# Local-attention scores at the head of a step, and transposes copied by two engines in turn

## The chip, the cores and the metric

The kernel runs on one core of one Trainium2 chip. The metric is the device time of a whole launch in microseconds. The version before the change takes 2577.65 us (median of 3 runs, 2576.64 to 2578.03). A core has a matrix engine (TensorE, "PE" in the profile, with its weight loads shown as "PEld"), VectorE (DVE), ScalarE (ACT), GpSimd (POOL) and SyncE (SP), which issues nearly all DMAs here. TensorE writes to PSUM, of which there are eight banks; DVE and ACT read PSUM and write SBUF.

## The reference, cut to what matters

Two layers on 512 tokens of width 1024. Each layer is a SwiGLU block, a token mix of three attention branches, and a second SwiGLU block, each followed by a layer norm. The change touches the token mix alone.

```python
def _token_mix(h, w_in, ...):
    q_a, kv_a, g_a, q_b, k_b, v_b, q_c, k_c, v_c, f_c = _split_cols(h @ w_in)
    o_a = _nsa(q_a, kv_a, g_a, ...)      
    o_b = _swa_sink(q_b, k_b, v_b, sinks, ...)  
    o_c = _fox(q_c, k_c, v_c, f_c, b_f)  
    g = jax.nn.sigmoid(h @ w_gate + b_gate).reshape(B, S, N_BRANCH, D)
    merged = g[:, :, 0] * (o_a @ w_br_a) + g[:, :, 1] * (o_b @ w_br_b) + g[:, :, 2] * (o_c @ w_br_c)
    return merged @ w_out
```

`_swa_sink` is local attention: a query block of 128 tokens sees its own block and the one before, with a bias and a sink in the softmax. `_fox` is causal attention with a decaying bias over all earlier blocks. `_nsa` has a compressed branch (its keys and values come from a small two-layer network over 32-token blocks, called the conv here), a selected branch and a window branch; with 512 tokens all eight blocks of 64 are selected, so both see all earlier tokens. Eight heads each, 64 wide, in pairs.

## The kernel before

All matrix products are done at nearly fp32 accuracy: a weight tile `raw` arrives by DMA, ACT rounds it to `hi` (L140), DVE forms the rest `lo` (L141), and one k of a projection is three matmuls of 512 columns (L161 to L163). The order of TensorE's and POOL's instructions is the order in which the program writes them; those of ACT, DVE and SP are ordered by the compiler's scheduler.

In `mix` (once per layer) the projections of the token mix are cut into *fillers*: `chunk` makes eight of them out of one projection of 128 columns, one per k, and appends them to the deque `fill`. `pump(n)` runs the next n. When the last filler of a chunk has run, its `then` starts the evacuation: `set_q` has ACT and DVE build a query tile `qs` in four instructions in turn (L403, L404) and makes the query known to the order two fillers or more later; `fox_k` and `nsa_k` build key tiles `ks` through DMAs; `set_v` transposes values. Entries marked `free` don't count: among them `feed`, which stands ahead of the fillers from the third query chunk on and issues the two loads of one conv weight `cw1` (L529) as long as fewer than four are under way. Other fillers are `m.cum` (a cumulative sum by matmuls, L483 and L486), `tr` (transposes `glT` in the conv, L550) and `conv2` (its last products `kv`, L582 and L585).

The attention is done by *units*: `Swa`, `Fox` and `Nsa`, each for one pair of heads and one query block. A unit has three parts:

- `s`, scores: matmuls into a PSUM tile of tag `sc` (three buffers), then bias, maximum, exponential and scale on DVE, ACT, and POOL or DVE (`norm`, L610). The result is `p`, in SBUF. It yields once for each of `nseg` segments: one for `Swa`, two for `Fox` and `Nsa`.
- `tr`, transposes: TensorE transposes `p` block by block into a PSUM tile of tag `tp` (two buffers; names ptS, ptF, ptN, ptC), and `ev_pt` copies each back to `p`. It yields after each group; `ngrp` is their number: one for `Swa`, two for `Fox`, three or five for `Nsa`.
- `pv`: the products with the values into one PSUM tile `po`.

`ev_pt(dst, src, n)` raises a counter that all callers share and gives the copy to DVE (L393) when n divides the counter, otherwise to ACT (L395); n = 0 is always ACT, and n = 1, for Nsa's compressed tile ptC, always DVE. The transposes of values (`vT`) use n = 2.

SBUF tiles of tag `p` have PB = 13 buffers: scores, the conv's inputs `z` (four), its weights `cw1` and `cw2`, and small ones such as `gl`, which holds the forget gate's logarithms until `cum` has run.

There are eight batches with two `Swa` units each, then for each of four head pairs one batch with four units and two with two. `step(cur, prev, n)` weaves three things into TensorE's stream: the scores of the batch `cur`, the transposes of the batch before (`prev`), and n fillers; then it does `pv` for `prev`, and behind it what `feed` has put into `narrow`, the conv's matmuls `hid` (L536). It first pumps until the queries and keys of `cur` exist. Two fillers are kept for the time between the last transposes and `pv`. The rest is spread over `slots`, the larger of the numbers of score segments `ns` and pairs of transpose groups `nt`; in a slot the scores come first, then fillers up to the slot's middle, then a pair of transpose groups, then fillers up to its end. For a Swa step ns was 2 and nt 1: two slots, the transposes in the second. `PUMPS` lists n for every step.

Of the kernel before, what the change touches and what calls it, by code (L numbers as in the profile page):

```python
# [18 lines left out]
P = 128  # L19
# [45 lines left out]
def body(tc, a, out, depth=DEPTH):  # L65
# [15 lines left out]
    def ps(tag=None, name="ps", shape=(P, 512)):  # L81
        if tag is None:
            tag = PS_ALL[ring[0] % 8]
            ring[0] += 1
        return psp.tile(list(shape), F32, name=name, tag=tag, bufs=PS_TAGS[tag])
# [266 lines left out]
    def mix(l, wts, pend, done_ffn, xap, xa, nxt):  # L352
# [35 lines left out]
        def ev_pt(dst, src, n):  # L388

            eng[0] += 1  # L390
            with tc.high_priority(100):
                if n and eng[0] % n == 0:
                    nc.vector.tensor_copy(dst, src)  # L393
                else:
                    nc.scalar.activation(dst, src, AF.Copy)  # L395
# [118 lines left out]
        def conv(ws):  # L514
# [52 lines left out]
            def end():  # L567
                while narrow or c.n < 16:
                    feed()
                    narrow.popleft()()  # L570
                tr()
# [40 lines left out]
        class Swa:  # L612
# [37 lines left out]
            def tr(u):  # L650
                pv = u.p.rearrange("p s (b q) -> p s b q", q=P)[:, :, 0:u.nb]
                pt = ps("tp", "ptS", (P, 2, 2, P))[:, :, 0:u.nb]
                for s in range(2):
                    for b in range(u.nb):
                        nc.tensor.transpose(pt[:, s, b], pv[:, s, b], ident)
                ev_pt(pv, pt, 4)
                yield

            def pv(u, po):
# [7 lines left out]
        class Fox:  # L667
# [33 lines left out]
            def tr(u):  # L701
                n = u.qb + 1
                for s in range(2):
                    pt = ps("tp", "ptF")[:, 0:n * P]
                    for b in range(n):
                        nc.tensor.transpose(pt[:, b * P:(b + 1) * P], u.p[s][:, b * P:(b + 1) * P], ident)
                    ev_pt(u.p[s][:, 0:n * P], pt, 0)
                    yield

            def pv(u, po):  # L710
# [6 lines left out]
        class Nsa:  # L717
# [83 lines left out]
            def tr(u):  # L801
                for s in range(2):
                    for p in u.n[s]:
                        pt = ps("tp", "ptN", (P, 2, 2, P))[:, 0:p.shape[1]]
                        for k in range(p.shape[1]):
                            for br in range(2):
                                nc.tensor.transpose(pt[:, k, br], p[:, k, br], ident)
                        ev_pt(p, pt, 3)
                        yield
                    if s == 0:  # L810
                        pc = u.pc.rearrange("p s n -> p (s n)")
                        pt = ps("tp", "ptC", (P, P))
                        nc.tensor.transpose(pt, pc, ident)
                        ev_pt(pc, pt, 1)
                        yield
# [100 lines left out]
        def pump(n=1):  # L916
            while n > 0 and fill:
                n -= fill.popleft()() is not FREE
# [30 lines left out]
        chunk(CKV + 2 * P, nsa_k(0))  # L949
        chunk(CKV + 4 * P, nsa_k(1))  # L950
        fill.append(tr)
        chunk(CQA, set_q(m.qa, 0))
        fill.insert(len(fill) - 2, lambda: conv2(cv))
# [23 lines left out]
        def need(u):  # L977
            if u.br == 1:
                return u.m in m.qb and hasattr(m, "kb")
            if u.br == 2:  # L980
                return u.m in m.qc and u.m in m.kc and u.m in m.vc and u.m in m.nck
            return u.m in m.qa and hasattr(m, "vbd") and hasattr(m, "kc2")
# [8 lines left out]
        def chain(gens):  # L991
            for g in gens:
                yield from g

        def step(cur, prev, n):


            for u in cur:
                while not need(u):
                    pump(1)  # L1000
                    n -= 1
            it, iu = chain(u.tr() for u in prev), chain(u.s() for u in cur)
            nt, ns = sum(u.ngrp for u in prev), sum(u.nseg for u in cur)
            pair = 2
            nt = (nt + pair - 1) // pair
            slots = max(nt, ns, 1)
            done = 0

            def upto(x):
                nonlocal done  # L1010
                x = int(round(x))
                if x > done:
                    pump(x - done)
                    done = x

            last = min(2, max(n, 0))
            n -= last
            for j in range(slots):
                if j * ns // slots != (j + 1) * ns // slots or slots == ns:
                    next(iu, None)  # L1020
                upto(n * (2 * j + 1) / (2 * slots))
                if j * nt // slots != (j + 1) * nt // slots or slots == nt:
                    for _ in range(pair):
                        next(it, None)
                upto(n * (j + 1) / slots)
            for _ in iu:
                pass
            for _ in it:
                pass
            pump(last)  # L1030
            if prev:
                po = ps("po", "po", (P, 4, P))
                for j, u in enumerate(prev):
                    u.pv(po[:, j])
                while narrow:
                    narrow.popleft()()
                for j, u in enumerate(prev):
                    nc.scalar.activation(o_t[u.br][u.m][:, u.qb * P:(u.qb + 1) * P], po[:, j], AF.Copy)

        PUMPS = [10] * 8 + [11, 10, 11] * 4 + [8]  # L1040
        for cur, prev, n in zip(batches + [[]], [[]] + batches, PUMPS):
            step(cur, prev, n)
        while fill:
# [40 lines left out]
        for d in range(KD):  # L1084
            g_t = gates0 if d == 0 else g_1 if d == 1 else gates(d)
            for br in (1, 2, 0):
# [3 lines left out]
                p = ps(name="brp")  # L1090
# [114 lines left out]
    for l in range(depth):  # L1205
        fin = l == depth - 1
        wts, pend, done = ffn(l, a["ffn1_w1"][l], a["ffn1_w2"][l], 0, xa, wts, pend, done, False, lambda: mix_first(l))
        wts, pend, done, xap, xa = mix(l, wts, pend, done, xap, xa, lambda: ffn_first(a["ffn2_w1"][l]))
        wts, pend, done = ffn(l, a["ffn2_w1"][l], a["ffn2_w2"][l], 2, xa, wts, pend, done, fin,
                              lambda: None if fin else ffn_first(a["ffn1_w1"][l + 1]))  # L1210
# [30 lines left out]
```

## Time and profile before

| | |
|---|---|
| median of the runs | 2577.65 us |
| the profiled execution's own time | 2576.7 us |
| its span, first to last instruction | 2575.0 us |
| granted TensorE clock, mean | 0.998 |
| DMA, mean | 104 GB/s, 268.97 MB |
| Swa steps of the first layer | about 428 to 517 us |
| Fox and Nsa steps of the first layer | about 517 to 712 us |
| the same of the second layer | about 1704 to 1793 and 1793 to 1988 us |

A row such as `458.52 0.63 PE L655 MATMUL ptS<-ident,p ... x4 [0.84 <-ACT p L395]` is read: at 458.52 us from the span's start, for 0.63 us, four matmuls of line 655 write ptS from ident and p; TensorE was idle 0.84 us before, until ACT's instruction of line 395 on tile p ended. In a list of groups, the busy time in us and the mean of one in ns stand between the two bars, and the idle time before the group with its releasers behind the second.

### The profile page before, as it was taken

What the parts mean: (1) busy time and instruction counts of PE and PEld (TensorE: products, weight loads), DVE (VectorE), ACT (ScalarE), POOL (GpSimd) and SP (SyncE); (2) the same over time, 40 slices, a digit from 0 to 9 for tenths busy, and PEclk for the clock granted to TensorE, in tenths of its full rate; (3) what the DMA queues carried; (4) which work ended last, traced back from release to release, by engine and by line L of the source; (5) the groups of instructions that cost most, each with busy time, mean ns of one, the idle gap of its engine ahead of it and who ended that gap; (6) DMA issues with size and microseconds to landing.
All of it is one profiled execution on the core that took longest, in us unless ns stands there. A gap on an engine that the chain in (4) does not pass through costs nothing. (4 is left out here: it accounts for less than half of the span.)

```text
span 2575.0 us, 34112 instructions
## 1 busy us (share of the span) xinstructions
PE 2544.7 (99%) x13099; PEld 2109.3 (82%) x13099; DVE 1197.1 (46%) x2565; ACT 949.3 (37%) x1947; POOL 184.4 (7%) x371
## 2 busy tenths in 40 slices
PE   9999999999999999999999999999999999999998
PEld 8888887788888888888888888877888888888887
DVE  4344245576654363332343432555766534543323
ACT  3222224477642332222232221345776323322211
POOL 0000001133300000000000000101332000000000
PEclk9999999999999999999999999999999999999999
DMA  6433334633143433333333332435321434233331
GB/s 213 119 94 95 98 92 127 172 82 83 50 139 99 122 99 98 98 98 92 113 90 98 96 94 97 129 102 156 95 75 42 143 103 142 81 97 98 99 92 63
DMA packets 375170, 268.97 MB, mean 104 GB/s; under 512 B 17384, under 2 KB 351272, under 8 KB 375008
## 3 DMA queue, kind: packets, MB, share of 16 engines
q1 hardware_dynamic: 373856, 262.61, 35.0%
q0 software_dynamic: 1152, 4.19, 0.4%
q8 instruction: 103, 1.69, 0.3%
q14 instruction: 59, 0.48, 0.1%
HBM read 247.83 MB, written 9.49 MB: 100 GB/s over the span
## 5 line engine op out<-in xcount | busy, mean ns | idle before, releaser
L141 DVE TENSOR_TENSOR lo<-raw,hi 128x1024 fp32r<-128x1024 f32 (+2 forms) x414 | 490.8, 1189 | 854.4 <-ACT hi L140 853.8
L140 ACT ACTIVATE hi<-raw 128x1024 fp32r<-128x1024 f32 (+2 forms) x414 | 424.4, 1031 | 1226.0 <-issue 696.4
L161 PE MATMUL pj<-xh,hi 128*128 128x512 f32 (+1 forms) x720 | 267.2, 371 | 1.5 <-ACT vt L448 1.4
L163 PE MATMUL pj<-xh,lo 128*128 128x512 f32 (+1 forms) x720 | 254.9, 354 | 0.4 <-DVE lo L141 0.4
L162 PE MATMUL pj<-xl,hi 128*128 128x512 f32 (+1 forms) x720 | 254.7, 354 | 0.0
L161 PE MATMUL pg<-xh,hi 128*128 128x512 f32 x640 | 249.7, 390 | 0.0
L162 PE MATMUL pg<-xl,hi 128*128 128x512 f32 x640 | 249.7, 390 | 0.0
L163 PE MATMUL pg<-xh,lo 128*128 128x512 f32 x640 | 249.5, 390 | 0.0
L163 PE MATMUL pu<-xh,lo 128*128 128x512 f32 x640 | 249.0, 389 | 0.0
L161 PE MATMUL pu<-xh,hi 128*128 128x512 f32 x640 | 249.0, 389 | 0.0
L162 PE MATMUL pu<-xl,hi 128*128 128x512 f32 x640 | 249.0, 389 | 0.0
L174 PE MATMUL acc<-hi,ha 128*128 128x512 f32 x576 | 227.3, 395 | 0.0
L175 PE MATMUL acc<-hi,ha 128*128 128x512 f32 x576 | 227.3, 395 | 0.0
L176 PE MATMUL acc<-lo,ha 128*128 128x512 f32 x576 | 227.2, 395 | 0.0
L286 DVE TENSOR_TENSOR t<-t,pu 128x512 f32<-128x512 f32 x80 | 55.0, 687 | 216.6 <-PE pu L163 216.6
L163 PEld LDWEIGHTS pj<-xh,lo 128*128 128x128 f32 x720 | 135.5, 188 | 20.5 <-DVE lo L141 0.6
L161 PEld LDWEIGHTS pj<-xh,hi 128*128 128x128 f32 x720 | 136.0, 189 | 17.0 <-issue 3.1
L162 PEld LDWEIGHTS pj<-xl,hi 128*128 128x128 f32 x720 | 136.2, 189 | 11.3 <-DVE xl L1187 0.2
L203 POOL TENSOR_SCALAR st<-st 128x1 f32<-128x1 f32 x24 | 8.4, 352 | 1890.4 <-ACT junk L201 1890.4
L163 PEld LDWEIGHTS pg<-xh,lo 128*128 128x128 f32 x640 | 120.6, 188 | 25.1
L162 PEld LDWEIGHTS pg<-xl,hi 128*128 128x128 f32 x640 | 120.5, 188 | 25.0
L161 PEld LDWEIGHTS pg<-xh,hi 128*128 128x128 f32 x640 | 120.5, 188 | 25.0
(244 smaller groups left out, 4322.9 us busy)
## 6 DMA issues: line engine op xcount, KB each, us to landing
raw<-in_ffn_w_dram SPq DMA_DIRECT2D x264, 512.0 KB, 3.8
raw<-in_w_in_dram SPq DMA_DIRECT2D x56, 512.0 KB, 4.0
raw<-in_w_gate_dram SPq DMA_DIRECT2D x48, 512.0 KB, 3.9
ks<-hl SPq DMA_DIRECT2D x96, 128.0 KB, 2.3
raw<-in_w_out_dram SPq DMA_DIRECT2D x16, 512.0 KB, 3.7
tab<-bvec SPq DMA_DIRECT2D x16, 256.0 KB, 2.8
x_sp<-xa POOLq DMA_DIRECT2D x8, 512.0 KB, 6.8
cw<-in_cmp_k_w_dram SPq DMA_DIRECT2D x32, 128.0 KB, 3.5
```

The lines of the kernel that those rows point to most:

```text
L140: nc.scalar.activation(hi[:, c], raw[:, c], AF.Copy)
L141: nc.vector.tensor_tensor(lo[:, c], raw[:, c], hi[:, c].bitcast(F32), op=OP.subtract)
L161: nc.tensor.matmul(o, hi[:, k], vh, start=first, stop=False)
L162: nc.tensor.matmul(o, hi[:, k], vl, start=False, stop=False)
L163: nc.tensor.matmul(o, lo[:, k], vh, start=False, stop=last)
L174: nc.tensor.matmul(o, sh(k)[:, t], hi[:, c], start=k == 0, stop=False)
L175: nc.tensor.matmul(o, sl(k)[:, t], hi[:, c], start=False, stop=False)
L176: nc.tensor.matmul(o, sh(k)[:, t], lo[:, c], start=False, stop=k == nk - 1)
L203: nc.gpsimd.tensor_scalar(st[:, 4:5], st[:, 3:4], 1.0 / D, EPS / ALPHA ** 2, op0=OP.mult, op1=OP.add)
L286: nc.vector.tensor_tensor(t, t, pu, op=OP.mult)
```

## The change

Three things, all in `mix`. The `n` of `ev_pt` becomes 2 for the transposes of all three kinds of units (before: 4 for Swa, 0 for Fox, 3 for Nsa; ptC keeps 1, vT its 2). In `step`, where the current batch has exactly two score segments in all, which is a batch of two Swa units, both are issued in one go: ns is halved, so there is one slot in place of two, with both scores at its head and the transposes in its middle. And `PUMPS` gives the first two steps 13 fillers in place of 10, the next six 9 in place of 10; their sum stays 80.

```diff
@@ Swa.tr
-                ev_pt(pv, pt, 4)
+                ev_pt(pv, pt, 2)
@@ Fox.tr
-                    ev_pt(u.p[s][:, 0:n * P], pt, 0)
+                    ev_pt(u.p[s][:, 0:n * P], pt, 2)
@@ Nsa.tr
-                        ev_pt(p, pt, 3)
+                        ev_pt(p, pt, 2)
@@ step
             nt = (nt + pair - 1) // pair
+            both = 2 if ns == 2 else 1
+            ns //= both
             slots = max(nt, ns, 1)
...
                 if j * ns // slots != (j + 1) * ns // slots or slots == ns:
-                    next(iu, None)
+                    for _ in range(both):
+                        next(iu, None)
...
-        PUMPS = [10] * 8 + [11, 10, 11] * 4 + [8]
+        PUMPS = [13, 13] + [9] * 6 + [11, 10, 11] * 4 + [8]
```

## The prediction

> **What bounds the kernel now.** I read the page's busy rows first, then the list of what TensorE waited for, then the two attention stages of each layer as windows, and last the order of instructions around each wait.
>
> ```profile
> PE 2544.7 (99%) x13099; PEld 2109.3 (82%) x13099; DVE 1197.1 (46%) x2565; ACT 949.3 (37%) x1947; POOL 184.4 (7%) x371
> ```
>
> TensorE is busy for 2544.7 of 2575.0 us. No edit takes a matmul away, so what can be won is TensorE's idle time, 30.3 us in all, and only the part that the change touches. The list of TensorE's waits (engine, line, what it waited for: us in total, times, longest) has all that matters:
>
> ```profile
> PE ptN L807 <- ACT p L395: 5.8, 8, 1.7
> ...
> PE sS L629 <- DVE qs L404: 2.7, 2, 1.3
> PE glT L550 <- DVE p L393: 1.7, 2, 0.9
> PE ptS L655 <- DVE p L610: 1.7, 2, 0.9
> PE ptS L655 <- ACT p L395: 1.7, 2, 0.8
> PE ptC L813 <- ACT p L395: 1.4, 2, 0.7
> ```
>
> Each comes an even number of times: once or more per layer, in the same place. The windows of the two layers bear this out (columns: PE, weight loads, DVE, ACT, POOL busy, granted clock, DMA share, GB/s). The first and third are the Swa steps, the others the Fox and Nsa steps:
>
> ```profile
> 420.00:517.00 97.00, 92.13 (x555) 71.62 (x552) 62.62 (x203) 50.73 (x142) 11.28 (x24) 1.00 0.57 155
> 517.00:712.00 195.00, 191.40 (x1431) 160.43 (x1432) 131.83 (x573) 136.26 (x458) 66.94 (x127) 1.00 0.26 70
> 1696.00:1793.00 97.00, 92.12 (x555) 71.74 (x553) 62.66 (x202) 50.77 (x142) 11.23 (x24) 1.00 0.57 155
> 1793.00:1988.00 195.00, 191.39 (x1432) 160.46 (x1433) 131.39 (x574) 136.40 (x459) 66.85 (x127) 1.00 0.26 70
> ```
>
> TensorE sits idle 4.9 us in a layer's Swa steps and 3.6 us in its Fox and Nsa steps; the clock is full. Whatever I work out for one layer counts twice.
>
> The list shows a little less than a wait costs, because a matmul's recorded end lies past the start of its successor when nothing stops it:
>
> ```profile
> 441.17 0.39 PE L163 MATMUL pj<-xh,lo 128*128 128x512 f32 x1
> 441.40 0.38 PE L655 MATMUL ptS<-ident,p 128*128 128x128 f32 x2
> 442.63 0.41 PE L655 MATMUL ptS<-ident,p 128*128 128x128 f32 x2 [0.85 <-DVE p L610]
> ```
>
> The first takes 0.39 us and the next starts 0.23 us after it, so 0.16 us is overlap. I add 0.16 us to every listed wait.
>
> **The order of the Swa steps, counted out.** A filler is one k of a projection, three matmuls of 0.23 us or 0.69 us. The fillers of a layer are numbered from the first step: 1 is the last of zk, 2-9 zv, 10-17 the second q chunk (qb1), 18-25 qb2, 26 `cum`, 27-34 qb3, 67 `tr`, 74 `conv2`. Before, a Swa step is: scores, 4 fillers, scores, 2 fillers, both transposes, 2 fillers, 2 more, then the products with v. After, it is both scores, 4 fillers (6 in the second step), both transposes, the other fillers, products. `both` acts only where two Swa units are current, which is eight steps; the sum of fillers is 80 in both versions, so from the ninth step on the order is the same. Steps 1 and 2 end at fillers 13 and 26 instead of 10 and 20.
>
> **Waits that this removes.**
>
> First, the transposes of the second step (the 0.85 us row above) stand behind a softmax scale that is late because DVE works through zv's additions. Scores to transposes: 12 fillers before; now scores at filler 0, transposes after filler 19. At 0.69 us that is 4.8 us more, which exceeds the wait. Removed: 1.7 + 2x0.16 = 2.0 us.
>
> Second, the third step's scores want qb1, which is made by ACT and DVE in turn after filler 17:
>
> ```profile
> 448.63 0.44 PE L629 MATMUL sS<-ks,qs 128*128 128x128 f32 x2
> 450.40 0.44 PE L629 MATMUL sS<-ks,qs 128*128 128x128 f32 x2 [1.33 <-DVE qs L404]
> ...
> 449.66 0.69 DVE L404 SCALAR_TENSOR_TENSOR qs<-pj,qs 64x512 fp32r<-64x512 f32 x1
> ```
>
> Before, step 3 starts at filler 20, three fillers later; now at filler 26, nine later, 4.1 us more. Removed: 2.7 + 2x0.16 = 3.0 us.
>
> Third, `cum` was filler 26 and lay just ahead of step 3's transposes, so three tiles asked for two `tp` buffers:
>
> ```profile
> 456.71 0.38 PE L483 MATMUL cum<-tri,gl 128*8 128x128 f32 x2
> 457.02 0.33 PE L655 MATMUL ptS<-ident,p 128*128 128x128 f32 x1
> ...
> 458.52 0.63 PE L655 MATMUL ptS<-ident,p 128*128 128x128 f32 x4 [0.84 <-ACT p L395]
> ```
>
> Now `cum` ends step 2 and four fillers, products and scores come before the next transposes. Removed: 1.7 + 2x0.16 = 2.0 us. Together **-7.0 us**.
>
> `tr`, filler 67, stays directly behind a step's transposes (step 7 is 63-71, its transposes after 66), and those were copied by ACT and DVE already (counts 11 and 12 of the shared counter, every fourth to DVE). I leave the 1.7 us of glT as they are.
>
> **Waits that it may add in the Swa steps.** The pool `p` has 13 buffers. In step 2, z holds 4, cw2 1, gl 1 (until `cum`), the four score tiles 4: three are left, and a step takes up to four conv weights (`feed`, from filler 18 on). Before, only three fillers of step 2 came after that point; the fourteenth tile was a score tile of step 3, and it did wait for `cum`:
>
> ```profile
> 457.69 0.42 DVE L605 CUSTOM_DVE_ANT_0 p<-sS,tab 128x256 f32<-128x256 f32 x1
> ...
> 461.83 1.09 PE L663 MATMUL po<-p,v 128*64 128x128 f32 x16
> 462.75 1.90 PE L536 MATMUL hid<-cw,z 128*64 128x256 f32 x16
> ...
> 448.38 0.51 SPq L529 DMA_DIRECT2D cw<-in_cmp_k_w_dram  x1
> 449.23 0.34 SPq L529 DMA_DIRECT2D cw<-in_cmp_v_w_dram  x1
> ...
> cw<-in_cmp_k_w_dram SPq DMA_DIRECT2D x16, 128.0 KB, 3.3
> cw<-in_cmp_v_w_dram SPq DMA_DIRECT2D x16, 128.0 KB, 2.8
> ```
>
> DVE wrote that score tile 0.7 us after `cum` had ended near 457.0, and TensorE never felt it. Now step 2 has fillers 18 to 26, so the fourteenth can be the fourth conv weight, whose load can start only when `cum` ends at the tail of step 2. Its second half is issued 0.85 us after its first and lands 2.8 us later, 3.65 us after `cum`. TensorE wants it after the products (0.92 us) and three quarters of a hid group (three quarters of 1.83), 2.3 us after `cum`. In the worst case it stands 1.35 us per layer, and what is queued behind it is TensorE's whole stream; in the best case a score tile waits again (0). I take the middle, 0.7: **+1.4 us**, ends 0 and 2.7. Later steps are one conv group earlier and have free buffers. The other loads of SP keep their order of need; a filler's weights are fetched a chunk ahead.
>
> `conv2` (filler 74) takes a `tp` buffer:
>
> ```profile
> 511.07 0.68 PE L585 MATMUL kv<-cw,glt 128*64 128x64 f32 x8
> ...
> 512.36 0.55 ACT L593 ACTIVATE vbd<-kv 32x128 f32<-32x128 f32 x2 [0.35 <-POOL vbd L579]
> ```
>
> It is read out 1.2 us after its matmuls end (512.91 against 511.75). Before, scores and two fillers lay between it and the transposes; now one filler, 0.69 us. The first transposes have the other buffer and take 0.4 us, so the second are short by 0.1 us at best, and by 1.3 us if the last two exponentials of that step's scores go ahead of it on ACT. I take 0.5: **+1.0 us**, ends 0 and 2.6.
>
> **The copies.** In the Fox and Nsa steps of one layer, 517 to 712 us (groups by line: busy us, mean ns of one, then the engine's idle time before them):
>
> ```profile
> L395 ACT ACTIVATE p<-ptF 128x128 f32<-128x128 f32 (+3 forms) x32 | 13.1, 432 | 7.9 <-PE ptF L706 6.6 <-POOL p L610 0.9
> L395 ACT ACTIVATE p<-ptN 128x512 f32<-128x512 f32 (+1 forms) x30 | 15.5, 516 | 5.6 <-PE ptN L807 5.5
> L393 DVE COPY p<-ptN 128x512 f32<-128x512 f32 (+1 forms) x18 | 10.8, 601 | 3.5 <-PE ptN L807 2.0 <-POOL p L610 1.3
> ```
>
> Counting through, 16 of the 32 ptF copies and 15 of the 30 ptN copies go to DVE, and 9 of the 18 go back to ACT; ptC (n = 1) stays on DVE and moves the shared counter on, so there are runs of three on one engine. ACT loses 6.6 + 7.8 and gains 4.7 us: 127 of 195. DVE gains 16.7 and loses 5.4 us: 143 of 195, the fuller of the two. The longest wait shows why ACT alone was late, and how DVE can be:
>
> ```profile
> 615.77 0.27 PE L813 MATMUL ptC<-ident,pc 128*128 128x128 f32 x1
> 617.69 0.52 PE L807 MATMUL ptN<-ident,p 128*128 128x128 f32 x3 [1.64 <-ACT p L395]
> ...
> 616.96 0.58 ACT L395 ACTIVATE p<-ptN 128x512 f32<-128x512 f32 x1
> ...
> 615.89 1.22 DVE L141 TENSOR_TENSOR lo<-raw,hi 128x1024 fp32r<-128x1024 f32 x1
> ...
> 617.45 0.28 DVE L393 COPY pc<-ptC 128x128 f32<-128x128 f32 x1
> ```
>
> All ten waits here (8 ptN, 2 ptC) are for an ACT copy: 7.2 + 10x0.16 = 8.8 us is the most that can go, 0 the least. With two buffers and alternate engines each run of three still has one copy on ACT, and the tile after it waits for that one; only the waits in which two ACT copies queued up shrink. I take half: **-4.4 us**. Against it stand copies that now queue behind a weight split on DVE; I take +1.0 us, from 0 to 3.7 (62 moved copies of both layers, a tenth of the window in such splits, 0.6 us left of one).
>
> A repeated gap on TensorE before a tile of two buffers bears on a rule of the Trainium skill (Perfetto Trace Analysis, Optimization Strategy): the same gap repeated on the engine that should be full can mean too few buffers for the next tile. By it the copier matters little, this term is 0 and the time that of the second rival below.
>
> **Sum:** -7.0 + 1.4 + 1.0 - 4.4 + 1.0 = -8.0 us. The profiled execution took 2576.7 us, 1.7 over its span and 0.95 under the median; 2568.7 for it is **2569.6 us** as a median.
>
> **Rivals.**
>
> All attacked waits go and none comes: -7.0 - 8.8, 2561.8 us. For it: ACT is the only releaser in the second stage. Against: ACT keeps half the copies.
>
> The copies win nothing, the two buffers being the cause: -7.0 + 2.4 + 1.0, 2574.0 us. For it: the wait at 617.69 is for one of a pair, and the pair's other copy will now be on ACT.
>
> Slower: DVE becomes what releases the `tp` buffers. Place: the Fox and Nsa steps. Mechanism: a copy stands behind a weight split, as the ptC of 615.77 did, copied 1.4 us after its matmul. If a quarter of the 62 moved copies are so late and TensorE stands 1.2 us for each, 15x1.2 = 18 us; with the Swa terms 2577.65 - 7.0 + 2.4 + 18 = 2591 us. It cancels the Swa gain from four such waits on, and shows as slower from nine. For it: DVE at 143 of 195 us. Against: no wait of TensorE in these steps is for DVE today, though it does 18 such copies and 16 of ptC per layer.
>
> A copy is also longer on DVE:
>
> ```profile
> L395 ACT ACTIVATE p<-ptN 128x512 f32<-128x512 f32 x40 | 23.6, 589 | 8.7 <-PE ptN L807 8.5
> ...
> L393 DVE COPY p<-ptN 128x512 f32<-128x512 f32 x24 | 16.6, 690 | 6.3 <-PE ptN L807 4.0 <-POOL p L610 1.3 <-POOL pc L610 1.0
> ```
>
> That is 0.10 us for the largest form, 6.3 us over 62 copies, of which the sum has none on TensorE's path, since DVE's 52 idle us a layer hold it. The Trainium skill (Perfetto Trace Analysis, Optimizing Scalar/DVE Operations) speaks against the move likewise: it puts the fixed cost of reading PSUM at about 125 ns on DVE and 51 on ScalarE. By those 74 ns, all on the path, 4.6 us (an estimate) would come off the gain, which would leave 3.4.
>
> **How the numbers follow.** 0.2% (5.2 us) is about what a measurement of this kernel tells from no change. Forecast 0.54, all waits gone 0.12, copies win nothing 0.23, slower 0.11. The first two are faster by more than that (below 2572.5) save for 0.02 of the forecast's own spread; the third is within it; the fourth above. So faster 0.64, same 0.25, slower 0.11. The forecast's own range is 2564 to 2575; the whole range goes from the second case (2561) to 2579, past the third with all its unknown costs at their upper ends (2574.0 + 1.3 + 1.6 + 2.7 = 2579.6).
>
> **What would show it.** In the changed profile the three Swa waits (ptS for L610, sS for L404, ptS for L395) are gone and glT's stays; a wait of hid L536 for a cw load shows the fourteenth buffer, one of ptS L655 near conv2's kv the `tp` clash. ptN and ptC waits for ACT about halve, with small ones for DVE copies at their side. DVE's busy time in the Fox and Nsa window is near 143 us and ACT's near 127. Wrong would be: DVE as releaser of most ptN waits, or a Swa window that still has more than 4 us idle.

## The result, and the profile after

The changed kernel takes 2569.17 us (median of 7 runs, 2565.98 to 2569.57). In the same comparison the kernel before takes 2576.47 us (7 runs, 2576.09 to 2578.03). The ratio is 0.9968, with a 95% interval of 0.9957 to 0.9980: faster by about 7 us. 2569.6 us was forecast. The profiled execution took 2569.09 us, against 2576.7 before.

The span is 2567.4 us. The matmuls are the same 13099 and are busy for 2545.5 us, as long as before (2544.7), so the time came out of TensorE's idle time. Its list of waits, after (us in total, times, longest):

```profile
PE ptN L807 <- DVE pc L393: 3.0, 2, 1.5
PE glT L550 <- DVE p L393: 1.7, 2, 0.9
...
PE ptS L655 <- ACT p L395: 0.9, 2, 0.5
PE ptN L807 <- ACT p L395: 0.9, 2, 0.5
PE ptC L813 <- ACT p L395: 0.4, 2, 0.2
```

The two waits of the Swa steps for L610 and L404 are not in it. glT's 1.7 us stand as before. What ptN and ptC waited for ACT copies was 5.8 + 1.4 us and is 0.9 + 0.4. But 3.0 us of ptN now stand under a DVE copy, ptS waits for an ACT copy in a new place, and a wait of hid for a load (0.2 us) is new. The two windows of the first layer that the prediction shows, after:

```profile
420.00:517.00 97.00, 94.57 (x574) 73.49 (x573) 63.74 (x209) 49.86 (x141) 13.98 (x26) 1.00 0.57 155
517.00:712.00 195.00, 192.76 (x1434) 162.03 (x1434) 139.96 (x594) 129.70 (x441) 65.67 (x125) 1.00 0.26 72
```

TensorE's idle time fell from 4.9 to 2.4 us in the one and from 3.6 to 2.2 us in the other. Windows at fixed times shift against the work when a kernel gets faster, so from here on a stage is cut where its work begins: the Swa stage from its first sS to the first sF, the Fox and Nsa stage from there to the first brp, in both layers. Before (the first number behind the window is its length; the row left out has 90.23 again):

```profile
428.51:518.74 90.23, 86.03 (x536) 67.56 (x535) 59.03 (x194) 47.94 (x138) 12.07 (x26) 1.00 0.57 155
518.74:718.11 199.37, 195.77 (x1446) 164.06 (x1445) 133.90 (x577) 140.70 (x467) 66.14 (x126) 1.00 0.26 70
...
1794.97:1994.10 199.13, 195.52 (x1446) 164.07 (x1445) 133.25 (x577) 140.62 (x467) 66.06 (x126) 1.00 0.26 71
```

and after:

```profile
429.93:517.60 87.67, 85.92 (x536) 67.76 (x535) 59.02 (x198) 44.99 (x134) 13.98 (x26) 1.00 0.59 161
517.60:715.18 197.58, 195.34 (x1447) 164.18 (x1445) 142.62 (x598) 132.52 (x445) 65.67 (x125) 1.00 0.25 71
1701.80:1789.08 87.28, 85.87 (x535) 67.75 (x534) 58.96 (x198) 44.99 (x134) 14.03 (x26) 1.00 0.59 161
1789.08:1986.66 197.58, 195.34 (x1446) 164.20 (x1445) 141.99 (x598) 132.66 (x445) 65.75 (x125) 1.00 0.26 71
```

The Swa stages won 2.56 + 2.95 = 5.5 us, the Fox and Nsa stages 1.79 + 1.55 = 3.3 us, 8.85 us together. The span fell by 7.6 us only. 1.4 of these were lost long before the changed code: the first Swa stage begins at 429.93 in place of 428.51. The windows of the same ten microseconds, before and then after, show it:

```profile
36.00:46.00 10.00, 10.00 (x48) 7.57 (x48) 6.39 (x10) 2.04 (x3) 0.00 (x0) 0.83 0.61 172
```

```profile
36.00:46.00 10.00, 10.00 (x40) 6.60 (x40) 6.38 (x10) 2.02 (x3) 0.00 (x0) 0.66 0.62 177
```

The granted clock was 0.66 in place of 0.83, so that 40 matmuls were done and not 48. The kernels do the same work there. In the profiles of before, after and the experiments below, which (but for the third `tp` buffer) differ in the token mix alone, the first Swa stage begins anywhere from 426.7 to 430.5 us, so this varies from execution to execution. The stage lengths leave it out; the totals don't.

### The profile page after: what moved, and what is told of

Same layout as the page of the kernel before. It is cut to its first block, busy times and chain, and to the rows that moved or that the text cites. A ratio compares the mean times of both kernels' runs of the same rounds, so it can differ in the third digit from the quotient of the medians.

```text
span 2567.4 us, 34066 instructions
## 1 busy us (share of the span) xinstructions
PE 2545.5 (99%) x13099; PEld 2110.8 (82%) x13099; DVE 1214.1 (47%) x2617; ACT 927.4 (36%) x1895; POOL 187.6 (7%) x371
## 4 chain that ended last, share of the span: by engine, by line
PE 97%; DVE 1%; ACT 1%; DMA 1%; issue 0%; POOL 0%; DVEq 0%; POOLq 0%; SPq 0%; ACTq 0%
PE acc L176 7%; PE acc L174 7%; PE acc L175 7%; PE pg L161 6%; PE pg L162 6%; PE pg L163 6%; PE pu L161 6%; PE pu L163 6%; PE pu L162 6%; PE pj L161 5%; PE pj L163 5%; PE pj L162 5%; PE gate L161 3%; PE gate L162 3%; PE gate L163 3%; PE brp L162 2%
## 5 line engine op out<-in xcount | busy, mean ns | idle before, releaser
L141 DVE TENSOR_TENSOR lo<-raw,hi 128x1024 fp32r<-128x1024 f32 (+2 forms) x414 | 490.3, 1188 | 852.0 <-ACT hi L140 851.3
```

The lines of the kernel that those rows point to most:

```text
L141: nc.vector.tensor_tensor(lo[:, c], raw[:, c], hi[:, c].bitcast(F32), op=OP.subtract)
```

## The experiments

Two theories were set against each other part by part. Mine was that of the prediction: the order and the fillers win in the Swa stage, the copies win in the Fox and Nsa stage, and the parts add up. The rivals were that only one part does the work, and that the two `tp` buffers, not the copying engine, set the waits.

**The copies alone** (kernel before, all three `ev_pt` with n = 2):

```diff
-                ev_pt(pv, pt, 4)
+                ev_pt(pv, pt, 2)
-                    ev_pt(u.p[s][:, 0:n * P], pt, 0)
+                    ev_pt(u.p[s][:, 0:n * P], pt, 2)
-                        ev_pt(p, pt, 3)
+                        ev_pt(p, pt, 2)
```

> Only the three ev_pt counts become 2; order and PUMPS as before. Theory (each edit acts in its own stage): TensorE's waits in the Fox and Nsa steps go as in the changed kernel, ptN and ptC standing 2.7 us a layer instead of 4.4, the Swa waits (ptS, sS, glT) stay; 3 to 4 us faster than before. Rival 1 (the order earns all of it, the copies nothing): Fox and Nsa waits unchanged within 0.5 us, time within 1 us of before. Rival 2 (DVE becomes the releaser): ptN waits for DVE copies of more than 5 us in all, slower.

Measured: 2576.20 us against 2576.99, ratio 0.9995 (0.9986 to 1.0004). No gain could be measured. The stage windows of this kernel say why:

```profile
428.13:518.88 90.75, 86.23 (x535) 67.55 (x534) 61.50 (x198) 46.02 (x134) 12.07 (x26) 1.00 0.57 155
518.88:716.51 197.63, 195.39 (x1446) 164.21 (x1445) 142.90 (x599) 132.50 (x445) 65.95 (x126) 1.00 0.26 71
1703.50:1795.81 92.31, 87.83 (x535) 68.70 (x534) 61.47 (x198) 46.01 (x134) 12.02 (x26) 0.98 0.56 152
```

In the Fox and Nsa stages the whole gain is there: 1.74 us here, 1.55 in the second layer's (197.58 us). The Swa stages gave back 0.5 and 2.1 us, and in the second layer the clock is at 0.98. The 0.5 us, in both layers, lies at step 2's products, which wait for a copy on DVE, and just ahead of step 3's scores. TensorE's timeline at step 3's scores in the second layer (the first layer's row, at 450.57, has the same 1.37 us):

```profile
1725.93 0.44 PE L629 MATMUL sS<-ks,qs 128*128 128x128 f32 x2 [1.37 <-DVE qs L404]
```

and the window just behind it:

```profile
1726.00:1730.00 4.00, 4.00 (x12) 3.19 (x13) 1.45 (x9) 0.97 (x5) 0.59 (x2) 0.57 0.90 273
```

There the clock fell to 0.57. In the first layer the same wait left it at 1.00 over the whole stage: the 1.6 us between the two Swa stages (92.31 and 90.75) are the price of the clock. So the copies are worth 3.3 us in one stage, and in this kernel the old Swa steps give most of it back.

**The order and the fillers, with the old copies** (the changed kernel, with n back at 4, 0 and 3):

> Both scores at the head and the new PUMPS; the copy counts as before (4, 0, 3). Theory: the three Swa waits (ptS for L610, sS for L404, ptS for L395 behind cum) go, small ones come (hid for a cw load, ptS behind conv2's kv), the Fox and Nsa waits stay at 4.4 us a layer; 5 to 6 us faster than before. Rival 1: the whole 8 us. Rival 3 (the Swa waits only move): under 2 us faster.

Measured: 2571.82 us, ratio 0.9981 (0.9973 to 0.9990), 5.2 us faster. The first layer's stages of this kernel:

```profile
426.72:514.25 87.53, 85.81 (x535) 67.77 (x534) 56.44 (x194) 46.93 (x138) 12.00 (x26) 1.00 0.59 160
514.25:713.65 199.40, 195.81 (x1447) 164.00 (x1445) 133.62 (x577) 140.59 (x467) 65.98 (x125) 1.00 0.25 70
```

The Swa stage is as short as in the changed kernel, the other as long as before. In this kernel each part keeps to its stage.

**The order alone** (the same, with PUMPS as before):

```diff
-        PUMPS = [13, 13] + [9] * 6 + [11, 10, 11] * 4 + [8]
+        PUMPS = [10] * 8 + [11, 10, 11] * 4 + [8]
```

> Only both scores at the head of a Swa step; PUMPS and copies as before. Theory: step 3 starts at filler 20 again, so sS still waits 1.5 us a layer for the query; cum, filler 26, now comes two fillers behind the transposes and its wait goes; tr, filler 67, comes three fillers behind them and the 1.0 us of glT go; conv2, filler 74, stands directly ahead of the transposes of step 8, which then wait 1 to 2 us. 1 to 3 us faster in all. Rival 4 (the order is what earns the Swa part): 5 us or more faster.

Measured: 2581.13 us, ratio 1.0016 (1.0007 to 1.0025): slower, against my expectation. The waits of the transposes in steps 2 and 3 and that of glT are gone, as expected. The waits for the queries are not. TensorE's timeline at step 3's scores in the first layer:

```profile
449.76 0.44 PE L629 MATMUL sS<-ks,qs 128*128 128x128 f32 x2 [1.94 <-DVE qs L404]
451.98 1.65 PE L629 MATMUL sS<-ks,qs 128*128 128x128 f32 x6 [1.77 <-DVE qs L404]
```

and the window behind them:

```profile
453.00:457.00 4.00, 4.00 (x12) 3.23 (x12) 2.17 (x16) 2.05 (x10) 0.23 (x1) 0.51 0.98 307
```

Step 3's scores stood 3.7 us a layer for the query, where 1.35 were listed before, and the clock fell to 0.51 behind them. Two reasons can be read off, counted from the first sS (428.51 before, 429.34 here). The stand in step 2 that the order removes had been time for the query too: TensorE is free for step 3's scores 1.5 us sooner. And the query is ready 0.7 us later (its last instruction on DVE ends at 451.92 here, at 450.35 before): ACT begins it at 448.42, behind all four exponentials of step 2, where it began at 445.22, ahead of them. Together that is the 2.3 us by which a layer's wait grew.

**The fillers alone** (kernel before, with the new PUMPS):

> Only the new PUMPS; two slots and the copy counts as before. Theory: the query wait of step 3, the late softmax of step 2 and the clash of cum with step 3's transposes all go by the filler numbers alone, hid waits for a cw load as in the changed kernel (0.3 to 0.7 us a layer), conv2 lies four fillers' work ahead of the transposes and costs nothing: 5 to 7.5 us faster than before, as much as order and fillers together or more. Rival 4: under 3 us faster.

Measured: 2572.54 us, ratio 0.9980 (0.9971 to 0.9989). Its Swa stages:

```profile
429.81:517.62 87.81, 85.99 (x536) 67.83 (x535) 59.36 (x194) 47.50 (x138) 14.57 (x26) 1.00 0.60 162
...
1704.05:1791.43 87.38, 85.85 (x536) 67.83 (x535) 59.46 (x194) 47.51 (x138) 14.60 (x26) 1.00 0.60 163
```

That is 175.2 us for both, and 175.1 with order and fillers: on top of the fillers, scores at the head add nothing. The six more fillers ahead of step 3 are what wins in the Swa stage, since they alone remove the wait for the query.

**One conv weight fewer at the start** (the changed kernel):

```diff
-                if c.n < 16 and len(narrow) < 4:
+                if c.n < 16 and len(narrow) < (3 if c.n <= 3 else 4):
```

> The changed kernel, but feed gives step 2 only three conv weights, so that no fourteenth tile asks for a buffer of p before cum has run. Theory (the wait of hid in step 2 is the fourteenth buffer): no hid wait for a cw load is left, the Swa stage of the first layer (first sS to first sF) is 0.6 us shorter than the changed kernel's 87.67, that of the second 0.3 shorter than 87.28. Rival (the loads are late for another reason, the DMA queue): hid still waits.

Measured: 2576.89 us, ratio to the kernel before 0.9997 (0.9987 to 1.0007), so the gain was gone. TensorE's timeline of this kernel in the first layer:

```profile
451.41 1.46 PE L536 MATMUL hid<-cw,z 128*64 128x256 f32 x12
...
503.77 0.61 PE L550 MATMUL glT<-ident,gl 128*128 128x128 f32 x2 [2.32 <-DVE gl L544]
```

and the window that begins at the second row:

```profile
503.00:508.00 5.00, 4.23 (x13) 3.45 (x14) 1.11 (x4) 0.17 (x1) 0.00 (x0) 0.66 1.20 229
```

The three weights of step 2 ran without a stand, so the fourth is the cause there. That it is its buffer, the changed kernel's list of what SP waited for shows; neither the kernel before nor this one has such a row:

```profile
SPq L529 <- PE cum L483: 6.8, 2, 3.4
```

But one weight was then left over for a step of its own, its load was late (1.28 us), `tr` waited 2.32 us for the conv's result, and the clock fell. The test answers its question, and its total says nothing about the price of the wait.

**The conv's last products two fillers earlier** (the changed kernel):

```diff
-        fill.insert(len(fill) - 2, lambda: conv2(cv))
+        fill.insert(len(fill) - 4, lambda: conv2(cv))
```

> The changed kernel with conv2 two fillers earlier, so that three fillers and not one lie between kv and the transposes of step 8. Theory (the ptS wait there is kv still holding a tp buffer): the 0.64 us of ptS go in both layers, Swa stages 0.6 us shorter. Rival (the copies of the transposes themselves are late): ptS still waits.

Measured: 2570.71 us, ratio 0.9973 (0.9962 to 0.9984). The wait near kv did not move. Timelines of TensorE, ACT and POOL of this kernel:

```profile
511.83 0.38 PE L655 MATMUL ptS<-ident,p 128*128 128x128 f32 x2
512.68 0.66 PE L655 MATMUL ptS<-ident,p 128*128 128x128 f32 x4 [0.47 <-ACT p L395]
...
515.27 0.53 ACT L593 ACTIVATE vbd<-kv 32x128 f32<-32x128 f32 x2
...
512.66 1.40 POOL L610 TENSOR_SCALAR p<-p,stS 128x256 f32<-128x256 f32 x3 [9.64 <-ACT p L395]
514.01 0.30 POOL L579 MEMSET vbd<- 128x256 f32 x1
```

kv's buffer is held until ACT has read it into vbd, and that waits for vbd's memset on POOL, which stands in program order behind the scales of both scores. So the second transposes take the buffer of the first, and wait for ACT's copy of these. Moving the matmuls of kv doesn't free the buffer.

**All copies to one engine** (the changed kernel with n = 1 for all three, and with n = 0 for all three; ptC stays on DVE in both):

> The changed kernel with every copy of a transpose of the three units on DVE. Theory (a late copy costs on whichever engine it queues, and two engines are better than one): ptN waits for DVE of 2 to 5 us a layer, Fox and Nsa stage (first sF to first brp) 198 to 201 us against 197.58. Rival (ACT's lateness was the whole cause): no ptN wait left, stage under 196.5.

> The changed kernel with every copy of a transpose of the three units on ACT (ptC stays on DVE). Theory: ptN waits for ACT of more than 4.4 us a layer, Fox and Nsa stage 199.5 to 202 us; Swa stage within 1 us of the changed kernel's. Rival (the number of tp buffers is the cause, not the copier): stage within 0.5 us of 197.58.

Measured: all on DVE 2572.07 us, ratio 0.9977 (0.9968 to 0.9987); all on ACT 2577.07 us, 0.9999 (0.9989 to 1.0008). The first Fox and Nsa stage, all on DVE:

```profile
517.53:716.34 198.81, 196.21 (x1446) 164.30 (x1445) 160.74 (x639) 116.48 (x404) 64.81 (x125) 1.00 0.26 70
```

with this wait at the head of those in the stage:

```profile
PE sN L765 <- DVE stN L605: 1.8, 2, 0.9
```

The same stage, all on ACT:

```profile
518.61:720.20 201.59, 197.52 (x1446) 165.32 (x1445) 123.93 (x558) 147.97 (x486) 67.07 (x125) 0.99 0.25 70
```

and its largest wait there:

```profile
PE ptC L813 <- ACT p L395: 5.0, 6, 1.7
```

The stage goes 201.6, 198.8 and 197.6 us for all on ACT, all on DVE and in turn. On ACT the copies come late themselves. On DVE they come mostly in time (ptN waits 1.5 us for them in the whole list), but sN now waits for the softmax on DVE that frees its `sc` buffers, 3.4 us in the whole list: most of the wait moved from transposes to scores.

**A third `tp` buffer**, taken from the scores (the changed kernel):

```diff
-    PS_TAGS = {"mm": 2, "sc": 3, "tp": 2, "po": 1}
+    PS_TAGS = {"mm": 2, "sc": 2, "tp": 3, "po": 1}
```

> The changed kernel with three PSUM buffers for transposes and two for scores. Theory of the two buffers (the second rival of the prediction: not who copies but how many tiles wait): the ptN and ptC waits of the Fox and Nsa stage go almost wholly, 2.7 us a layer; but scores may wait for their own two, so that the stage is 195 to 199 us. Theory of the copier: a third buffer leaves more than 1 us a layer of ptN waits. The Swa stage gets longer by some us, since the conv's hid holds one of two score buffers.

Measured: 2620.36 us, ratio 1.0166 (1.0150 to 1.0181); the first Fox and Nsa stage took 224.4 us. Its largest wait:

```profile
PE sN L765 <- DVE stN L605: 17.3, 22, 1.5
```

No wait of ptN or ptC is left, so the rival is right that the buffers make these waits possible. Scores with two buffers then wait far more. The rule that the prediction draws from the Trainium skill (Perfetto Trace Analysis, Optimization Strategy), that a repeated gap can mean too few buffers, agrees with the waits that went; that the copier then matters little does not, by the stage lengths above.

**Copies by place** (the changed kernel; Fox always ACT, Nsa always DVE, Swa in turn):

```diff
-                    ev_pt(u.p[s][:, 0:n * P], pt, 2)
+                    ev_pt(u.p[s][:, 0:n * P], pt, 0)
-                        ev_pt(p, pt, 2)
+                        ev_pt(p, pt, 1)
```

> The changed kernel with Fox's copies all on ACT and Nsa's all on DVE, Swa's in turn. Theory (a copy costs where its engine is late at that moment: ACT while it does the exponentials of the next scores, which is when Nsa's transposes come): the 1.6 us wait of ptN for one ACT copy goes, Fox and Nsa stage 195.5 to 197.3 us against 197.58. Rival (only an even share counts): stage 198 us or more, as with all copies on DVE (198.8 and 199.2).

Measured: 2568.21 us, ratio 0.9965 (0.9951 to 0.9979). Both Fox and Nsa stages take 197.21 us, 0.37 less than in turn. The 1.5 us wait of ptN is gone, and small ones stand in its place. The totals can't tell this kernel from the changed one, since the two intervals overlap; the stages can.

**The Swa waits together** (the changed kernel; feed limits of 3, 4 and at the end 5, `tr` and `conv2` earlier, and `conv2`'s evictions ahead of others in the scheduler):

```diff
-                if c.n < 16 and len(narrow) < 4:
+                if c.n < 16 and len(narrow) < (3 if c.n <= 3 else 5 if c.n >= 11 else 4):
...
+            with tc.high_priority(100):
...
-        fill.append(tr)
+        fill.insert(len(fill) - 6, tr)
-        fill.insert(len(fill) - 2, lambda: conv2(cv))
+        fill.insert(len(fill) - 4, lambda: conv2(cv))
```

> The changed kernel with three repairs of the Swa stage: conv weights in groups of 3, 4, 4 and 5, so that no fourteenth tile waits for cum and the conv still ends in step 5; tr two fillers later; conv2 two fillers earlier and its four evictions at the priority of the transposes' copies. Theory: the hid wait (0.3 to 0.7 us), glT's 1.0 and the 0.64 of ptS go in both layers; Swa stages near 85.3 us against 87.67 and 87.28, 4 us faster than the changed kernel. Rival (a wait taken away there comes back behind the next tile, as with the conv weights in groups of three): Swa stages not under 87 us.

Measured: 2566.75 us, ratio 0.9960 (0.9947 to 0.9972), Swa stages of 86.28 and 86.17 us. The waits of glT and of step 2's hid are gone; the ptS wait of 0.47 us near kv is still there, so the priority did not help it. The Swa stages stay about 0.9 us above the 85.3 us that were expected, and the rival is partly right: step 4, which has five weights now, stands instead. Its twenty hid matmuls take 2.90 us (474.29 to 477.19) and 3.07 in the second layer, where sixteen take 1.83. SP issues the fifth weight at 474.10 only, behind the first of the products (SP's list has two waits of L529 for po, 8.4 us).

**All together** (that without the priority, the copies by place, and vbd's tile and memset moved from `conv2` to `tr`):

```diff
+                m.vbd = at.tile([P, 2, P], F32, name="vbd")
+                nc.gpsimd.memset(m.vbd, 0.0)
...
-            m.vbd = at.tile([P, 2, P], F32, name="vbd")
-            nc.gpsimd.memset(m.vbd, 0.0)
```

> The repairs of the Swa stage of e9_combo (without the raised priority), the copies of e11_byplace, and the memset of vbd moved from conv2 to tr, ahead of the scales of step 8's scores on POOL. Theory (the ptS wait of step 8 is vbd's evictions behind a memset that stands behind the scores' scales in POOL's queue): the 0.64 us of ptS go, Swa stage 85.4 to 85.8 us against 86.28 and 86.17, Fox and Nsa stage 197.2 as in e11_byplace; 2564.5 to 2566 us in all. Rival (ACT would be late for those evictions anyway): ptS still waits 0.6 us, Swa stage 86.2.

Measured: 2564.41 us (5 runs, 2563.80 to 2566.61) against 2576.58, ratio 0.9951 (0.9937 to 0.9965). This is the fastest version, below both kernels. The first layer's stages:

```profile
430.41:516.34 85.93, 85.45 (x535) 67.77 (x534) 58.93 (x198) 45.02 (x134) 14.00 (x26) 1.00 0.60 164
516.34:713.57 197.23, 195.98 (x1447) 164.33 (x1445) 147.86 (x606) 127.77 (x437) 64.73 (x125) 1.00 0.26 71
```

The timelines of TensorE and ACT near kv:

```profile
509.93 0.38 PE L655 MATMUL ptS<-ident,p 128*128 128x128 f32 x2
510.71 0.66 PE L655 MATMUL ptS<-ident,p 128*128 128x128 f32 x4 [0.41 <-ACT vbd L593]
...
510.13 0.53 ACT L593 ACTIVATE vbd<-kv 32x128 f32<-32x128 f32 x2
```

kv is now read out from 510.13, ahead of the second transposes, which then start at 510.71; with the memset behind the scales that was at 515.27, 2.6 us after them. So the memset on POOL held the buffer, but TensorE hardly gains: the second transposes start 0.78 us after the first, where it was 0.85 with the memset in its old place. ACT reads kv only after the four exponentials of that step's scores (until 510.04), and with the buffer held it is ACT's copy of the first transposes that comes behind them. The rival, that ACT would be late anyway, was right: the ptS wait did not go, and the Swa stages of 85.93 and 86.18 us miss the expected 85.4 to 85.8. Of the 0.35 us won in the first layer 0.26 lies in hid, not here.

## Why the prediction was right

**The sum.** -8.0 us was forecast. The stage lengths give -8.85 and the medians -7.3. That 2569.17 us came out within half a us of the forecast is in part luck: the Swa terms were off by up to 1.6 us, with both signs, and the start of the kernel varies by more than the gap. The terms, in us over both layers, the Swa ones counted from start to start of the matmuls:

| term | predicted | measured |
|---|---|---|
| the three Swa waits | -7.0 | -8.6 |
| fourteenth `p` buffer, hid | +1.4 | +2.0 |
| conv2 and `tp`, ptS | +1.0 | +1.4 |
| `cum` behind step 2's copies | not foreseen | +0.3 |
| the remainder | not foreseen | -0.6 |
| Swa stages, net | -4.6 | -5.5 |
| copies, Fox and Nsa stages, net | -3.4 | -3.3 |

The remainder is what the stage lengths leave over. It lies in gaps of a tenth of a us and less where one kind of matmul follows another; with both scores in one group there are fewer such places.

**The three Swa waits** went as predicted, and were worth more than the list showed, because two of them had a second, shorter stand beside them that the sum left out. Step 2's transposes, before:

```profile
443.25 0.44 PE L655 MATMUL ptS<-ident,p 128*128 128x128 f32 x2 [0.22 <-POOL z L500]
443.45 0.48 PE L161 MATMUL pj<-xh,hi 128*128 128x512 f32 x1
```

From the start of the first transposes (441.40, in the prediction) to the next projection went 2.05 us before. After, the six transposes of that step go as one group from 444.78 to 445.36: 0.58 us. That is 1.5 us a layer, not the 1.0 of the sum. The query's wait is 1.7 us a layer by the same count, with a short stand ahead of step 3's first scores, not 1.5. The eight transposes of step 3 took 1.88 us before and 0.79 after: 1.1 us, not 1.0. These sizes are off; the mechanism stands. What removes the waits, the experiments show: that for the query goes with the fillers alone, and the other two go with either the order or the fillers.

**The fourteenth buffer** came where it was expected. The timelines of TensorE and SP around step 2's end, after:

```profile
449.32 0.39 PE L163 MATMUL pj<-xh,lo 128*128 128x512 f32 x1
449.80 0.39 PE L483 MATMUL cum<-tri,gl 128*8 128x128 f32 x2
...
452.07 0.88 PE L663 MATMUL po<-p,v 128*64 128x128 f32 x12
452.78 2.25 PE L536 MATMUL hid<-cw,z 128*64 128x256 f32 x14
455.21 0.65 PE L536 MATMUL hid<-cw,z 128*64 128x256 f32 x2 [0.17 <-DMA cw<-in_cmp_v_w_dram]
455.78 1.19 PE L629 MATMUL sS<-ks,qs 128*128 128x128 f32 x8
...
452.86 0.34 SPq L529 DMA_DIRECT2D cw<-in_cmp_v_w_dram  x1
```

SP issues the second half of the fourth weight at 452.86 and the first at 452.17, just behind `cum`, whose last matmuls are recorded until 452.14. The sixteen hid matmuls take 3.00 us from 452.78 to 455.78, where the same sixteen took 1.83 before (462.75 to 464.58): 1.17 us of stand, and 0.80 in the second layer. The listed 0.2 us shows a fraction of it, since the profile files the rest as part of the group. The middle of the range was too low. That the fourth weight causes it was shown with one weight fewer, and SP's wait for `cum` names the buffer.

The first two rows show the stand that the prediction missed. `cum` starts 0.48 us after its predecessor, where it was 0.32 before (454.43 to 454.75): its `tp` buffer waits for the copy of step 2's transposes, now only six fillers back, which ends on DVE at 449.75. With the fillers alone these are four fillers back, and `cum` stands 0.6 us for ACT's copy.

**conv2 against the transposes** cost 0.70 us a layer (1.27 us for the six transposes, from 511.13 to the next projection, where 0.57 is usual), against 0.5. That kv holds a buffer was right. The reason given, the last exponentials ahead of its readers on ACT, was right but not the whole: the order of the Swa steps also put both scores' scales ahead of vbd's memset on POOL. The exponentials alone are enough for the stand: with the memset moved, the transposes still take 1.20 us.

**glT's wait** stayed at 1.7 us, by the reason given: it stands right behind the transposes in both kernels. `tr` two fillers later removes it.

**The copies** gave -3.3 us where -3.4 was forecast. The two terms behind it are less exact than their sum. The ten listed waits of 7.2 us became six of 4.3 us, so by the prediction's own count 3.5 us went and not 4.4, and of the +1.0 for copies that queue on DVE about 0.2 is left over. DVE and ACT were put at 143 and 127 us in the window; they are at 140.0 and 129.7. One expectation failed: the waits on DVE copies are not small, they are the longest left, 3.0 of the 3.9 us of ptN, and the prediction had named DVE as releaser of most ptN waits as a sign of being wrong. The timelines of TensorE, DVE and ACT, after, at the place that waited 1.64 us before:

```profile
613.55 0.27 PE L813 MATMUL ptC<-ident,pc 128*128 128x128 f32 x1
615.31 0.63 PE L807 MATMUL ptN<-ident,p 128*128 128x128 f32 x4 [1.48 <-DVE pc L393]
...
614.87 0.28 DVE L393 COPY pc<-ptC 128x128 f32<-128x128 f32 x1
...
614.69 0.58 ACT L395 ACTIVATE p<-ptN 128x512 f32<-128x512 f32 x1
```

DVE's copy ends at 615.15, ACT's at 615.27, and TensorE starts at 615.31. The list's name is right: in all five profiles with this wait TensorE starts 0.146 to 0.148 us behind DVE's copy. Behind ACT's it starts 0.042 to 0.047 us, and in no listed wait of these runs for ACT does it start sooner than 0.052 us after it. DVE made this copy late: it split a weight (L141) from 613.25 to 614.47, and Fox's softmax came next. That is the mechanism of the slower rival, in one place of a layer; it costs little there, because the ACT copy that TensorE waited for before was as late (1.64 us). ACT still holds the other buffer until 615.27, so the run of three with one copy on ACT that the prediction described is there too, and the wait goes when Nsa's copies all go to DVE.

The slower rival's time did not come about even with every copy on DVE: the stages took 198.8 and 199.2 us, against 199.4 and 199.1 before. Nor did the copies' longer time on DVE, in the rows or by the figures of the Trainium skill (Perfetto Trace Analysis, Optimizing Scalar/DVE Operations), show on TensorE's path: the stage won what was forecast without it.

**What the forecast treated as independent is not.** Its terms add up in the changed kernel, but alone the copies win nothing in total and the new order loses: both keep or lengthen the wait for step 3's queries, behind which the clock can fall, and the extra fillers remove it.

Not tried: the fillers with the new copies and the old order. The stages suggest the time of the changed kernel for it.

## What to carry to other kernels

When one engine bounds and the rest is small waits, cut the span where the work begins and ends, and cost a wait from start to start of its neighbours; a list of waits can show a sixth of what a place loses (0.2 of 1.17 us here). A buffer is held until its last reader has run, so look for what that reader waits for, a memset on a third engine for example, before moving the matmuls that fill it; and look for what comes next, since here the buffer came free 5 us sooner and TensorE won 0.07 us. Where two engines share a job, give each the places in which its own queue is short; taking turns is a good second (0.37 us a stage behind).

## What the hardware showed that was not expected

A wait of TensorE of 1.4 us can cost more than its own length again in clock: 1.37 us in the second layer of the copies-alone kernel cost another 1.6. The granted clock was 0.57 behind it (window from 1726), 0.51 behind 1.94 and 1.77 us with less than half a us of matmuls between them with the order alone, and 0.66 behind 1.28 and 2.32 us with one weight fewer. The same 1.37 us in the other layer cost no clock. Nor did waits of 1.33 and 1.64 us in the kernel before, while 1.66 us with all copies on ACT did (0.68 in the window 617 to 622). The Trainium skill (TensorE: Matmul & The Clock Gate, HAM oscillation) puts the limit at idle gaps of more than about 3.4 us. Here gaps that were each well under that were enough, in pairs and in two kernels nearly alone, though not every time; that a free-running window decides, as the same page says in its Part 1, would fit both outcomes, and no run here shows that window itself.
